# A hybrid attention trunk on one core: two groups of transposes move from TensorE to VectorE, two small matmul runs are merged, and one decay step is cut into even pieces

## The chip, the core and the metric

One core of a Trainium2 chip runs the whole kernel as one program. The metric is the device time of one execution in microseconds (us), median of several runs. TensorE is the matrix engine (PE in the rows, its weight loads PEld), VectorE is DVE, ScalarE is ACT, GpSimd is POOL, SyncE (SP) issues the weight DMAs. SBUF is the on-chip memory of 128 partitions, PSUM the accumulator memory that TensorE writes.

## What is computed

Batch 1, 256 tokens, width 2048, one layer, all in 32-bit floats. Cut to what matters:

```
h = rmsnorm(x);  z = h @ w_in         # q,k,v,gates of three branches, merge gates
a = gated linear attention (4 heads, key 128, value 256, chunked, key-wise decay)
a = rmsnorm(a) * silu(gate_a)          # 256 x 1024: "the gated attention's output"
b = forgetting attention (8 heads of 64, softmax with a forget bias) * silu(gate_b)
c = attention into 256 memory tokens (4 heads of 128) * silu(gate_c)
y = sum over the 3 branches of sigmoid(merge_i) * (branch_i @ w_branch_i)   # 256 x 2048
x = x + y @ w_out;  out = rmsnorm(x)
```

A matmul here takes its left operand with the contracted dimension on the partitions, so `a` and `y`, which come out with the tokens on the partitions, have to be transposed before they are multiplied by w_branch and w_out.

## The kernel before

**The stream.** Every large product is a stream of weight blocks of 2048 x 512 (`ORDER`). A block comes in 4 DMAs of 1 MB (`raw`), and is used in 8 pieces of 2 k-tiles. Each piece is split in two: ScalarE casts `hi` (line 173), VectorE subtracts to get `lo` (line 186), and TensorE forms hi*h1 + lo*h1 + hi*h2 in the format fp32r (lines 223 to 225 in `natural`, 253 and 258 in `transposed`, 1119 to 1121 for w_out). In `natural` a k-tile takes 6 matmuls of 512 columns, a piece 12. `w_kts` writes the cast of piece n+3 and the subtraction of piece n+2 into the program when TensorE's piece n comes; `hi` and `lo` have 4 buffers each.

**The lanes.** All other work is written as Python generators in three lists, `post`, `side` and `main`. After every k-tile `pull()` takes one step of the first generator in each list, so a step's instructions stand between two k-tiles in the order of every engine; `yield n` skips n-1 pulls, and `gap(n)` is a generator that only waits n pulls. Engines run their own instructions in this written order and wait for each other by semaphores.

**The places that the change touches.**
- `gla_scores` (from line 587): the key-wise decay is handled in three steps of block sizes 32, 8, 2. In the first one (`li == 0`) the scores of one 128-token block are three products with 32 rows each and 96, 64 and 32 columns (line 732), each in its own 32-column strip of the array; the later steps have four products of 48 columns. VectorE and ScalarE copy the results to `gA` (line 751).
- `fox` (from line 787): the forgetting attention goes over pairs of heads in a pipeline: `scores` (line 806, contraction 64, so half of the array's rows), softmax, `trans` (line 830, TensorE transposes), `moved` (line 834, VectorE copies to SBUF), `values` (line 842, 64 output rows, so half of the array's columns).
- `to_T` (line 921): for the two 512-wide halves of the gated attention's output `G["o"]`, eight times two TensorE transposes of 128 x 128 into PSUM (line 930), then ScalarE (933) and VectorE (934) make the two parts of `oT`. It runs in `post` right behind the gate of its half.
- `y_to_T` (line 1020): per 512-wide block n of y, two groups of four TensorE transposes (line 1030), then ScalarE (1032) and VectorE (1033) make the two parts of `yT`. It runs in `post` while the next block's first merge gate streams; the last one runs while w_out streams.
- `memory` (line 871), which is not changed, runs beside the first `to_T`: per head scores (904), maximum (906), exponential (910), norm (913, 915), transposes (895), copy (899), values (886).

Of the kernel before, what the change touches and what calls it, by code (L numbers as in the profile page):

```python
# [48 lines left out]
C_GAIN, C_MGAIN, C_BGK, C_GLAG, C_BF, C_N = 0, 16, 32, 36, 38, 39  # L49
# [10 lines left out]
def body(ctx, tc, xw, memT, xn, memn, wall, wsm, wup, cst, fgain, out):  # L60
    nc = tc.nc
    MM = nc.tensor.matmul
# [27 lines left out]
    def att():  # L90
        return ps_att.tile([P, NB], F32, tag="att", name=nm("att"))
# [27 lines left out]
    def gap(n):  # L119
        yield n  # L120
# [73 lines left out]
    def w_block():  # L194
        i = nblk[0]
        nblk[0] += 1
        return i

    def w_kts(i, group=1):

        for p in range(8):
            n = 8 * i + p
            if p % group == 0:
                w_cast(n + 3)
            if group == 1:
# [249 lines left out]
    G = {}  # L455
# [147 lines left out]
    def gla_scores():  # L603
# [79 lines left out]
        ps = att()  # L683
# [7 lines left out]
        for li in range(len(STEPS) + 1):  # L691
            s = STEPS[li] if li < len(STEPS) else None
            Qs = []
            if s:
                E = prep_keys(s)
                yield 2
                nc.scalar.activation(E, E, AF.Exp, scale=1.0 / 16)
                Qs.append(prep_queries(s, 0))
                yield 2
                nc.vector.tensor_tensor(out=E, in0=E, in1=gkf, op=ALU.mult)  # L700
                nc.scalar.activation(Qs[0], Qs[0], AF.Exp, scale=1.0 / 16)
                yield 2
                Qs.append(prep_queries(s, 1))
                yield 2
                nc.scalar.activation(Qs[1], Qs[1], AF.Exp, scale=1.0 / 16)
                times_q(Qs[0], s, 0)
                yield 2
                times_q(Qs[1], s, 1)
                yield 3
            else:  # L710
                E = gkf
                for half in range(2):
                    Qs.append(prep_pairs(half))
                yield 2
                for half in range(2):
                    nc.scalar.activation(odd(Qs[half]), odd(Qs[half]), AF.Exp, scale=1.0 / 16)
                yield 2
                for half in range(2):
                    times_odd(Qs[half], half)
                yield 2  # L720

            if li == 0:
                pss = [att().rearrange("p (e i) -> p e i", e=4) for _ in range(2)]
                off, n_q = (0, 96, 160), 3
            else:
                ps = att()[:, :8 * 48].rearrange("p (e i) -> p e i", e=8)
                off, n_q = (0, 48, 96, 144), 4
            for e in range(8):
                for j in range(n_q):
                    n = 96 - 32 * j if li == 0 else 48  # L730
                    dst = pss[e // 4][:, e % 4, P - n:] if li == 0 else ps[:, e, :]
                    MM(dst[32 * j:32 * j + 32], lhsT=E[:, e * P + 32 * j:e * P + 32 * j + 32],  # L732
                       rhs=Qs[e // 4][:, e % 4, off[j]:off[j] + n], start=True, stop=True,
                       skip_group_check=True)
            if li == 0:
                places = []
            elif s:
                m = gmask[li - 1][:, :, :8 // s or 1]
                places = [(gD.rearrange("p e (b s) -> p e b s", s=4 * s)[:, :, :, (b + 1) * s:],
                           m[:, b:b + 1, :].unsqueeze(3),  # L740
                           ps[:, :, (0, 24, 40)[b]:(24, 40, 48)[b]].rearrange("p e (b s) -> p e b s", s=(3 - b) * s))
                          for b in range(3)]
            else:
                places = [(gD.rearrange("p e (b s) -> p e b s", s=2)[:, :, :, 1], gpair[:, :, :16], ps[:, :, :16]),
                          (gD, gdiag[:, :, :32], ps[:, :, 16:])]
            yield 1
            if li == 0:
                for j in range(3):
                    q = slice(32 * j, 32 * j + 32)
                    for c in range(2):  # L750
                        (nc.scalar.copy if j == 1 else nc.vector.tensor_copy)(
                            gA[q, 4 * c:4 * c + 4, q.stop:], pss[c][q, :, q.stop:])
            for dst, mask, src in places:
                nc.vector.copy_predicated(dst, mask.bitcast(U32).to_broadcast(list(src.shape)), src)
            yield 2
# [34 lines left out]
    def fox():  # L790
# [45 lines left out]
        def values(p):  # L836

            po = att()
            for a, b, j, sl in ((0, S, 0, slice(0, S)), (P, S, 1, slice(S, 3 * P))):
                for e in range(2):  # L840
                    h = 2 * p + e
                    MM(po[64 * e:64 * e + 64, a:b], lhsT=fv[:, j, h * 64:(h + 1) * 64], rhs=pts[h][:, sl],
                       start=(j == 0), stop=(j == 1), skip_group_check=True)
            return po


        for k in range(6):
            this, last = (2 * k, 2 * k + 1), (2 * k - 2, 2 * k - 1)
            if k >= 2:
                po = values(k - 2)  # L850
                yield 1
                nc.scalar.copy(ob[:, k - 2, :], po[:, :S])
            if 1 <= k < 5:
                for h in last:
                    trans(h)
                yield 1
                for h in last:
                    moved(h)
                yield 1
            if k < 4:  # L860
                scores(k)
                yield 1
                for h in this:
                    masked(h)
                yield 1
                for h in this:
                    exps(h)
                yield 2
                for h in this:
                    normed(h)  # L870
                yield 2


    def memory():
# [43 lines left out]

    oT = [None] * 4

    def to_T(first, src, gain):

        for c in range(4):
            ct = first + c
            g, k = ct // 4, ct % 4
            if oT[g] is None:
                oT[g] = hpool.tile([P, 4, 2, S], F32R, tag=f"m12_{g}", name=nm("oT"))
            ps = att()
            for t in range(NT):
                nc.tensor.transpose(ps[:, t * P:(t + 1) * P], src(c, t), ident)  # L930
            yield 1
            sc = gain(c)
            nc.scalar.activation(oT[g][:, k, 0, :], ps[:, :S], AF.Copy, scale=sc)
            nc.vector.scalar_tensor_tensor(out=oT[g][:, k, 1, :], in0=ps[:, :S], scalar=sc,
                                           in1=oT[g][:, k, 0, :].bitcast(F32), op0=ALU.mult, op1=ALU.subtract)

    def silu_gate(dst, rstd):

# [69 lines left out]
    for cc in range(2):  # L1008
        gate = silu_gate(lambda t, cc=cc: G["o"][t][:, cc * NB:(cc + 1) * NB],
                         lambda cc=cc: G["rstd"][:, :, 2 * cc:2 * cc + 2])  # L1010
        post.append(gate)
        post.append(to_T(4 * cc, lambda c, t, cc=cc: G["o"][t][:, cc * NB + c * P:cc * NB + (c + 1) * P],
                         gain=lambda c: cs[:, C_GLAG + c % 2:C_GLAG + c % 2 + 1]))
    silu_gate_T("ob", 2)
    silu_gate_T("om", 3)
    main.drain()
# [4 lines left out]
    def y_to_T(n, y):  # L1021
        yield 2
        for c2 in range(2):
# [3 lines left out]
            for c in range(2):  # L1027
                for t in range(NT):
# [4 lines left out]
            nc.vector.tensor_tensor(out=yt[:, :, 1, :], in0=ps, in1=yt[:, :, 0, :].bitcast(F32),  # L1033
                                    op=ALU.subtract)

    def open_gate(ps, gt_):
        for t in range(NT):
            yield 1
            nc.scalar.activation(gt_[:, t, :], ps[t], AF.Sigmoid, scale=xcol[:, t:t + 1])
# [10 lines left out]
    for n in range(4):  # L1050
        gates = []
        for br in range(3):
            ps = natural(x12, range(KT), w_kts(w_block()))
            gates.append(a4([P, NT, NB]))
            post.append(open_gate(ps, gates[br]))
        src = w_kts(w_block())
        for br in range(3):
            kts = BR_KT[br]
            ps = natural(oT, kts, (next(src) for _ in kts))
            post.append(gated(br, ps, gates[br], gates[0]))  # L1060
        yT.append([])
        post.append(y_to_T(n, gates[0]))


    xr = []
# [189 lines left out]
```

## Time and profile before

| | |
|---|---|
| three runs | 803.58, 803.72, 804.22 us; median 803.72 |
| the profiled execution | 803.53 us |
| its span (first to last instruction) | 801.8 us, so 1.7 us lie around it |
| busy share of the span | TensorE 99%, weight loads 83%, VectorE 61%, ScalarE 51%, GpSimd 2% |
| TensorE's granted clock | 0.997 of full speed (2.4 GHz) over the span |
| chain that ended last | TensorE 95%, VectorE 2%, ScalarE 1% |
| DMA | 158.9 MB, mean 198 GB/s |

Busy time of TensorE is modelled as overlapping: a matmul of 512 columns is shown with 0.39 us, yet the next one starts 0.23 us later. So this document prices TensorE's work by distances between starts. Some matmuls stand twice in the trace: one of plain 32-bit operands is recorded as two.

### The profile page before, as it was taken

The page shows a single profiled execution, that of the slowest core. Times are in us where ns is not written, and L with a number is a line of the kernel's source. Part 1 is how long each engine was busy: PE and PEld are TensorE (multiplying, and loading weights), DVE is VectorE, ACT ScalarE, POOL GpSimd, SP SyncE. Part 2 cuts the span into 40 slices and gives each one's busy share as a digit, 9 for nine tenths or more (in the row PEclk, how much of TensorE's full clock was granted, in tenths as well). Part 3 has the DMA queues.
Part 4 walks back from the last instruction along what each step waited for, and adds up shares of the span by engine and source line. Part 5 has one row for each costly group of instructions (what it writes and reads, how often), then busy time and mean ns, then how long its engine had stood idle before and what let it go on. Part 6 is the DMA issues. An engine that isn't in the chain of part 4 may idle for free.

```text
span 801.8 us, 10259 instructions
## 1 busy us (share of the span) xinstructions
PE 792.7 (99%) x4064; PEld 663.5 (83%) x4064; DVE 486.7 (61%) x667; ACT 406.5 (51%) x562; POOL 15.3 (2%) x33
## 2 busy tenths in 40 slices
PE   9999999999999999999999999999999999999996
PEld 7888888888888788888888888888888888888886
DVE  6767978854757476676446644564447544575653
ACT  6768665654445475655444444444444444444632
POOL 5000000001000000000000000000000000000000
PEclk9999999999999999999999999999999999999998
DMA  9955747555544444455565565564555555548632
GB/s 325 387 200 184 251 163 296 168 205 185 204 158 158 158 158 158 158 203 185 190 209 182 186 202 176 200 208 165 204 198 177 204 182 188 207 164 296 248 132 106
DMA packets 27072, 158.90 MB, mean 198 GB/s; under 512 B 2984, under 2 KB 4528, under 8 KB 10128
## 3 DMA queue, kind: packets, MB, share of 16 engines
q1 hardware_dynamic: 26880, 158.22, 56.4%
q8 instruction: 32, 0.52, 0.3%
q14 instruction: 16, 0.13, 0.1%
q10 hardware_dynamic: 144, 0.02, 0.0%
HBM read 156.13 MB, written 2.11 MB: 197 GB/s over the span
## 4 chain that ended last, share of the span: by engine, by line
PE 95%; DVE 2%; ACT 1%; issue 1%; DMA 0%; SPq 0%; DVEq 0%
PE acc L223 19%; PE acc L225 19%; PE acc L224 19%; PE acc L253 13%; PE acc L258 7%; PE acc L1120 4%; PE acc L1119 4%; PE acc L1121 4%; PE att L253 2%; PE att L258 1%; DVE lo L186 1%; PE att L732 0%; PE att L442 0%; DMA xw<-xw 0%; PE att L1030 0%
## 5 line engine op out<-in xcount | busy, mean ns | idle before, releaser
L186 DVE TENSOR_TENSOR lo<-raw,hi 128x1024 fp32r<-128x1024 f32 x256 | 312.0, 1222 | 204.6 <-ACT hi L173 204.4
L173 ACT CAST hi<-raw 128x1024 fp32r<-128x1024 f32 x256 | 266.4, 1052 | 308.9 <-PE acc L225 239.9
L223 PE MATMUL acc<-hi,x 128*128 128x512 f32 x544 | 214.5, 394 | 0.0
L224 PE MATMUL acc<-lo,x 128*128 128x512 f32 x544 | 212.0, 390 | 0.0
L225 PE MATMUL acc<-hi,x 128*128 128x512 f32 x544 | 212.0, 390 | 0.0
L225 PEld LDWEIGHTS acc<-hi,x 128*128 128x128 f32 x544 | 102.1, 188 | 21.6
L223 PEld LDWEIGHTS acc<-hi,x 128*128 128x128 f32 x544 | 102.2, 188 | 21.1 <-issue 0.7
L224 PEld LDWEIGHTS acc<-lo,x 128*128 128x128 f32 x544 | 102.2, 188 | 20.8 <-DVE lo L186 0.4
L253 PE MATMUL acc<-x,hi 128*128 128x512 f32 x384 | 107.1, 400 | 0.0
L253 PEld LDWEIGHTS acc<-x,hi 128*128 128x128 f32 x384 | 66.3, 189 | 10.7 <-issue 1.0
L258 PEld LDWEIGHTS acc<-x,lo 128*128 128x128 f32 x384 | 58.8, 189 | 8.2
L258 PE MATMUL acc<-x,lo 128*128 128x256 f32 x384 | 61.0, 280 | 0.0
L225 PE MATMUL acc<-hi,oT 128*128 128x512 f32 x128 | 49.8, 389 | 0.0
L224 PE MATMUL acc<-lo,oT 128*128 128x512 f32 x128 | 49.8, 389 | 0.0
L223 PE MATMUL acc<-hi,oT 128*128 128x512 f32 x128 | 49.8, 389 | 0.0
L1119 PE MATMUL acc<-hi,a 128*128 128x512 f32 x96 | 37.5, 391 | 0.0
L1121 PE MATMUL acc<-hi,a 128*128 128x512 f32 x96 | 37.4, 389 | 0.0
L1120 PE MATMUL acc<-lo,a 128*128 128x512 f32 x96 | 37.4, 389 | 0.0
L223 PEld LDWEIGHTS acc<-hi,oT 128*128 128x128 f32 x128 | 24.0, 188 | 5.0
L224 PEld LDWEIGHTS acc<-lo,oT 128*128 128x128 f32 x128 | 24.0, 188 | 5.0
L225 PEld LDWEIGHTS acc<-hi,oT 128*128 128x128 f32 x128 | 24.0, 188 | 5.0
L1121 PEld LDWEIGHTS acc<-hi,a 128*128 128x128 f32 x96 | 18.0, 188 | 3.8
(222 smaller groups left out, 726.2 us busy)
## 6 DMA issues: line engine op xcount, KB each, us to landing
raw<-wall SPq DMA_DIRECT2D x130, 1024.0 KB, 4.8
a<-xn SPq DMA_DIRECT2D x8, 512.0 KB, 8.9
xw<-xw SPq DMA_DIRECT2D x4, 768.0 KB, 6.6
xw<-xw SPq DMA_DIRECT2D x7, 384.0 KB, 5.6
a<-memT SPq DMA_DIRECT2D x4, 512.0 KB, 5.8
a<-memn SPq DMA_DIRECT2D x4, 512.0 KB, 7.4
lraw<-wall SPq DMA_DIRECT2D x2, 1024.0 KB, 8.0
out<-a SPq DMA_DIRECT2D x8, 256.0 KB, 2.5
```

Of the source, the lines that this page charges most:

```text
L173: nc.scalar.copy(hi, raws[q][:, 2 * s:2 * s + 2, :])
L186: nc.vector.tensor_tensor(out=lo, in0=raws[q][:, 2 * s:2 * s + 2, :], in1=parts[n][0].bitcast(F32), op=ALU.subtract)
L223: MM(ps[t], lhsT=h1, rhs=hi, start=(kt == first), stop=False)
L224: MM(ps[t], lhsT=h1, rhs=lo, start=False, stop=False)
L225: MM(ps[t], lhsT=h2, rhs=hi, start=False, stop=(kt == last))
L253: MM(ps[c], lhsT=hi[:, c * P:(c + 1) * P], rhs=h_of(h, kt).rearrange("p a s -> p (a s)"), start=(kt == 0), stop=False, skip_group_check=True)
L258: MM(ps[c][:, :S], lhsT=lo[:, c * P:(c + 1) * P], rhs=h_of(h, kt)[:, 0, :], start=False, stop=(kt == KT - 1), skip_group_check=True)
L1119: MM(ps, lhsT=h1, rhs=hi, start=(kt == 0), stop=False)
L1120: MM(ps, lhsT=h1, rhs=lo, start=False, stop=False)
L1121: MM(ps, lhsT=h2, rhs=hi, start=False, stop=(kt == KT - 1))
```

## The change

Four edits. (1) `to_T` no longer uses TensorE: VectorE transposes 32 x 32 squares from SBUF to SBUF, 16 instructions per token tile of 128, so 32 per half and 64 in all (each 32 partitions x 4 squares, 128 elements per partition); the lines that make `oT` then read SBUF. It now runs in `side`, 10 pulls behind its gate, two squares per pull. (2) For y blocks 0 to 2 `y_squares` does the same with 16 instructions per block (32 partitions x 8 squares, 256 elements), one per pull, in `main`, 10 pulls after the block's end; block 3 keeps TensorE. (3) `fox`: `values` of pair k-2 now stands right in front of `scores` of pair k, behind `trans` and `moved`. (4) The first decay step's three products of 96, 64, 32 columns become four of 64, 64, 32, 32: the last 32 columns of the first go into the fourth strip.

```diff
             if li == 0:
                 pss = [att().rearrange("p (e i) -> p e i", e=4) for _ in range(2)]
-                off, n_q = (0, 96, 160), 3
+                todo = [(0, 0, 32, 96, 0), (1, 1, 64, P, 96), (2, 2, 96, P, 160), (3, 0, 96, P, 64)]
             else:
                 ps = att()[:, :8 * 48].rearrange("p (e i) -> p e i", e=8)
-                off, n_q = (0, 48, 96, 144), 4
+                todo = [(j, j, 0, 48, 48 * j) for j in range(4)]
             for e in range(8):
-                for j in range(n_q):
...
+                for j, k, a, b, off in todo:
+                    dst = pss[e // 4][:, e % 4, a:b] if li == 0 else ps[:, e, :]
+                    MM(dst[32 * j:32 * j + 32], lhsT=E[:, e * P + 32 * k:e * P + 32 * k + 32],
+                       rhs=Qs[e // 4][:, e % 4, off:off + b - a], start=True, stop=True,
                        skip_group_check=True)
...
         for k in range(6):
             this, last = (2 * k, 2 * k + 1), (2 * k - 2, 2 * k - 1)
-            if k >= 2:
-                po = values(k - 2)
-                yield 1
-                nc.scalar.copy(ob[:, k - 2, :], po[:, :S])
             if 1 <= k < 5:
                 for h in last:
                     trans(h)
@@
                 for h in last:
                     moved(h)
                 yield 1
+            if k >= 2:
+                po = values(k - 2)
             if k < 4:
                 scores(k)
-                yield 1
+            yield 1
+            if k >= 2:
+                nc.scalar.copy(ob[:, k - 2, :], po[:, :S])
+            if k < 4:
                 for h in this:
                     masked(h)
...
-                yield 2
+                yield 3 if k >= 2 else 2
...
+    def squares_T(dst, src, kts, ts):
+        v = src.rearrange("p t (k c i) -> p k t c i", c=4, i=32)
+        u = dst.rearrange("p k (t r j) -> p k t r j", r=4, j=32)
+        for r in range(4):
+            for c in range(4):
+                nc.vector.transpose(u[32 * c:32 * c + 32, kts, ts, r, :], v[32 * r:32 * r + 32, kts, :, c, :])
+                yield 1
+
+    def to_T(g, gain):
+        z = a4([P, 4, S])
+        for t in range(NT):
+            for i, _ in enumerate(squares_T(z, G["o"][t][:, g * NB:(g + 1) * NB].unsqueeze(1), slice(0, 4),
+                                            slice(t, t + 1))):
+                if i % 2:
+                    yield 1
...
-        post.append(to_T(4 * cc, lambda c, t, cc=cc: ...
+        side.append(gap(10))
+        side.append(to_T(cc, lambda c: cs[:, C_GLAG + c % 2:C_GLAG + c % 2 + 1]))
...
+    def y_squares(n, y):
+        z = a4([P, 4, S])
+        yield from squares_T(z, y, slice(0, 4), slice(0, NT))
+        for c2 in range(2):
...
+        if n == 0:
+            side.drain()
...
-        post.append(y_to_T(n, gates[0]))
+        if n < 3:
+            main.append(gap(10))
+            main.append(y_squares(n, gates[0]))
+        else:
+            post.append(y_to_T(n, gates[0]))
```

**TensorE's order in `fox`, pair k = 3.** Before, `values` of pair 1 (L842) stands eight stream matmuls ahead of `trans` of pair 2 (L830), and `scores` of pair 3 (L806) comes twelve stream matmuls behind that:

```order
L842 MATMUL att_2429<-b_2326,a_1767 64x256
L842 MATMUL att_2429<-b_2328,a_1767 64x256
L842 MATMUL att_2429<-b_2326,a_1767 64x128
L842 MATMUL att_2429<-b_2328,a_1767 64x128
L253 MATMUL acc_2255<-x_35_261,hi_2330 128x512 x2
L253 MATMUL acc_2255<-x_35_261,hi_2332 128x512 x2
L258 MATMUL acc_2255<-x_35_261,lo_2348 128x256 x2
L258 MATMUL acc_2255<-x_35_261,lo_2378 128x256 x2
L830 MATMUL att_2449<-ident,b_2358 128x128 x3
L830 MATMUL att_2453<-ident,b_2362 128x128 x3
```

Now the two stand together, behind `trans`:

```order
L225 MATMUL acc_2466<-hi_2406,x_6_116 128x512
L842 MATMUL att_2479<-b_2318,a_1777 64x256
L842 MATMUL att_2479<-b_2320,a_1777 64x256
L842 MATMUL att_2479<-b_2318,a_1777 64x128
L842 MATMUL att_2479<-b_2320,a_1777 64x128
L806 MATMUL att_2484<-a_1280,a_1029 128x128
L806 MATMUL att_2485<-a_1280,a_1029 128x128
L806 MATMUL att_2484<-a_1280,a_1029 128x256
L806 MATMUL att_2485<-a_1280,a_1029 128x256
L223 MATMUL acc_2465<-hi_2406,x_6_116 128x512
```

Nothing of the stream stands between `values` and `scores` any more. The number of matmuls is the same, and it is so for two pairs, k = 2 and k = 3. The second `scores` matmul takes a PSUM buffer that the first of the two `moved` copies (VectorE) frees.

**VectorE's order beside the memory attention**, from the middle of the fourth gate block (`lo` is the stream's subtraction L186, `a_1878`/`a_1888` and `a_1879`/`a_1889` the two halves of the attention's output, `msum` and `mmx` the memory attention's sums and maxima). Before:

```order
L186 TENSOR_TENSOR lo_2944<-raw_2793,hi_2930 128x1024
L957 TENSOR_TENSOR a_1878<-a_1878,b_2882 128x512
L186 TENSOR_TENSOR lo_2971<-raw_2793,hi_2932 128x1024
L957 TENSOR_TENSOR a_1879<-a_1879,b_2883 128x512
L899 COPY b_2984<-att_2966 128x512
L906 TENSOR_REDUCE mmx<-att_2986 128x2
L907 TENSOR_SCALAR mmx<-mmx 128x2
L186 TENSOR_TENSOR lo_3008<-raw_2845,hi_2990 128x1024
L934 SCALAR_TENSOR_TENSOR oT_3002<-att_3003,cs,oT_3002 128x256
L934 SCALAR_TENSOR_TENSOR oT_3002<-att_3020,cs,oT_3002 128x256
L186 TENSOR_TENSOR lo_3038<-raw_2845,hi_2992 128x1024
```

Now, the same stretch:

```order
L186 TENSOR_TENSOR lo_2956<-raw_2794,hi_2940 128x1024
L930 STREAM_TRANSPOSE a_2802<-a_1889 32x4x32 x2
L970 TENSOR_TENSOR a_1888<-a_1888,b_2884 128x512
L930 STREAM_TRANSPOSE a_2802<-a_1889 32x4x32 x2
L186 TENSOR_TENSOR lo_2987<-raw_2794,hi_2942 128x1024
L970 TENSOR_TENSOR a_1889<-a_1889,b_2885 128x512
L930 STREAM_TRANSPOSE a_2802<-a_1889 32x4x32 x2
L901 COPY b_3002<-att_2982 128x512
L930 STREAM_TRANSPOSE a_2802<-a_1889 32x4x32 x2
L908 TENSOR_REDUCE mmx<-att_3004 128x2
L909 TENSOR_SCALAR mmx<-mmx 128x2
L186 TENSOR_TENSOR lo_3024<-raw_2843,hi_3008 128x1024
```

Two squares stand between nearly every two of the old instructions. From the copy of the second head's transposes to the last subtraction of this weight block there are 20 of them, and 28 in the second half's stretch, from the first to the last subtraction of the first merge block.

## Rows read from the trace of the kernel before

**Rows 1.** The page: busy time, share of the span and instructions of each engine; and the chain of work that ended last, shares of the span by engine.

```profile
PE 792.7 (99%) x4064; PEld 663.5 (83%) x4064; DVE 486.7 (61%) x667; ACT 406.5 (51%) x562; POOL 15.3 (2%) x33
...
PE 95%; DVE 2%; ACT 1%; issue 1%; DMA 0%; SPq 0%; DVEq 0%
```

**Rows 2.** All waits of TensorE in the span: who was waited for, us in total, times, longest.

```profile
PE att L354 <- DVE ones L346: 1.1, 1, 1.1
PE att L253 <- DVE x L360: 0.5, 1, 0.5
```

**Rows 3.** The page's groups of the stream's two preparing instructions: out<-in, sizes, count | busy us, mean ns of one | idle time of the engine just before them, and what ended most of it.

```profile
L186 DVE TENSOR_TENSOR lo<-raw,hi 128x1024 fp32r<-128x1024 f32 x256 | 312.0, 1222 | 204.6 <-ACT hi L173 204.4
L173 ACT CAST hi<-raw 128x1024 fp32r<-128x1024 f32 x256 | 266.4, 1052 | 308.9 <-PE acc L225 239.9
```

**Rows 4.** Timeline of TensorE around the first four transposes of y block 0: start us, duration us, instruction, count.

```profile
448.62 0.39 PE L223 MATMUL acc<-hi,x 128*128 128x512 f32 x1
...
450.43 0.39 PE L225 MATMUL acc<-hi,x 128*128 128x512 f32 x1
450.66 0.60 PE L1030 MATMUL att<-ident,a 128*128 128x128 f32 x4
...
451.33 0.40 PE L224 MATMUL acc<-lo,x 128*128 128x512 f32 x1
```

**Rows 5.** The same around the first two transposes of the gated attention's output.

```profile
291.06 0.39 PE L225 MATMUL acc<-hi,x 128*128 128x512 f32 x1
291.29 0.38 PE L930 MATMUL att<-ident,a 128*128 128x128 f32 x2
...
291.74 0.40 PE L224 MATMUL acc<-lo,x 128*128 128x512 f32 x1
```

**Rows 6.** Timeline of TensorE at the first decay step (columns 96, 64, 32; the row names the first form) and at the second (columns 48), each with the stream's next matmuls.

```profile
110.17 1.51 PE L732 MATMUL att<-a,a 128*32 128x96 f32 x48
111.60 1.21 PE L253 MATMUL acc<-x,hi 128*128 128x512 f32 x4
...
134.25 0.89 PE L732 MATMUL att<-a,a 128*32 128x48 f32 x64
135.07 0.98 PE L253 MATMUL acc<-x,hi 128*128 128x512 f32 x3
```

**Rows 7.** Timeline of TensorE around one run of `scores` (L806) and one of `values` (L842) in the forgetting attention.

```profile
236.67 0.64 PE L258 MATMUL acc<-x,lo 128*128 128x256 f32 x4
237.14 1.09 PE L253 MATMUL acc<-x,hi 128*128 128x512 f32 x4
238.07 0.63 PE L258 MATMUL acc<-x,lo 128*128 128x256 f32 x4
238.63 0.93 PE L806 MATMUL att<-a,a 64*128 64x128 f32 x8
...
247.54 0.64 PE L258 MATMUL acc<-x,lo 128*128 128x256 f32 x4
248.10 0.87 PE L842 MATMUL att<-b,a 128*64 128x256 f32 x8
248.91 1.20 PE L253 MATMUL acc<-x,hi 128*128 128x512 f32 x4
```

**Rows 8.** Timeline at pair k = 3: VectorE's two copies of the transposes (L834), and TensorE's next `scores`.

```profile
251.95 1.01 DVE L834 COPY b<-att 128x384 f32<-128x384 f32 x2
...
253.91 0.93 PE L806 MATMUL att<-a,a 64*128 64x128 f32 x8
```

**Rows 9.** VectorE's groups by shape, for prices: 128, 256, 512 and 1024 elements per partition with two tensors read, then a copy of 32 partitions and a scaling by a column, both of 256 elements.

```profile
L639 DVE TENSOR_TENSOR a<-a 128x128 f32<-128x128 f32 x6 | 1.7, 286 | 0.0
L639 DVE TENSOR_TENSOR a<-a 128x256 f32<-128x256 f32 x6 | 2.5, 418 | 0.0
L1044 DVE TENSOR_TENSOR a<-acc,a 128x512 f32<-128x512 f32 x24 | 16.4, 683 | 0.0
L628 DVE TENSOR_TENSOR a<-a 128x1024 f32<-128x1024 f32 x3 | 3.7, 1219 | 0.0
L758 DVE COPY a<-b 32x256 f32<-32x256 f32 x2 | 0.6, 279 | 0.0
L915 DVE TENSOR_SCALAR b<-b,msum 128x256 f32<-128x256 f32 x8 | 2.5, 351 | 0.1
```

**Rows 10.** Timeline of VectorE: two such copies in a row, which write different groups of 32 partitions, and two such scalings in a row, which write all 128.

```profile
174.12 0.57 DVE L758 COPY a<-b 32x256 f32<-32x256 f32 x2
...
296.84 0.62 DVE L915 TENSOR_SCALAR b<-b,msum 128x256 f32<-128x256 f32 x2
```

**Rows 11.** VectorE's busy time in two stretches: from, to; length, busy us, instructions; then granted clock, DMA share, GB/s.

```profile
302.00:324.00 22.00, 14.46 (x24) 1.00 0.37 137
348.00:369.50 21.50, 15.37 (x16) 1.00 0.58 196
```

**Rows 12.** Timeline: the last subtraction of the fourth gate block (VectorE) and its first use (TensorE, L258); the last subtraction of the first merge block (the first of two in its row) and its first use (TensorE, L224).

```profile
322.81 1.22 DVE L186 TENSOR_TENSOR lo<-raw,hi 128x1024 fp32r<-128x1024 f32 x1
324.78 0.40 PE L258 MATMUL acc<-x,lo 128*128 128x256 f32 x2
...
368.41 2.35 DVE L186 TENSOR_TENSOR lo<-raw,hi 128x1024 fp32r<-128x1024 f32 x2
373.36 0.39 PE L224 MATMUL acc<-lo,x 128*128 128x512 f32 x1
```

More of the change, by code (lines that the diff above doesn't have):

```diff
@@ L723, in gla_scores @@
                 pss = [att().rearrange("p (e i) -> p e i", e=4) for _ in range(2)]
-                off, n_q = (0, 96, 160), 3
+                todo = [(0, 0, 32, 96, 0), (1, 1, 64, P, 96), (2, 2, 96, P, 160), (3, 0, 96, P, 64)]
             else:
                 ps = att()[:, :8 * 48].rearrange("p (e i) -> p e i", e=8)
-                off, n_q = (0, 48, 96, 144), 4
+                todo = [(j, j, 0, 48, 48 * j) for j in range(4)]
             for e in range(8):
-                for j in range(n_q):
[L730 to L733, printed above, removed]
+                for j, k, a, b, off in todo:
+                    dst = pss[e // 4][:, e % 4, a:b] if li == 0 else ps[:, e, :]
+                    MM(dst[32 * j:32 * j + 32], lhsT=E[:, e * P + 32 * k:e * P + 32 * k + 32],
+                       rhs=Qs[e // 4][:, e % 4, off:off + b - a], start=True, stop=True,
                        skip_group_check=True)
@@ L747, in gla_scores @@
             if li == 0:
-                for j in range(3):
-                    q = slice(32 * j, 32 * j + 32)
+                for j, k, a, b, _ in todo:
                     for c in range(2):
-                        (nc.scalar.copy if j == 1 else nc.vector.tensor_copy)(
-                            gA[q, 4 * c:4 * c + 4, q.stop:], pss[c][q, :, q.stop:])
+                        (nc.scalar.copy if j % 2 else nc.vector.tensor_copy)(
+                            gA[32 * k:32 * k + 32, 4 * c:4 * c + 4, a:b], pss[c][32 * j:32 * j + 32, :, a:b])
             for dst, mask, src in places:
@@ L919, in body @@
     oT = [None] * 4
-    def to_T(first, src, gain):
-        for c in range(4):
[L924 to L930, printed above, removed]
+    def squares_T(dst, src, kts, ts):
[12 more added lines that the diff above has]
+                    yield 1
+        oT[g] = hpool.tile([P, 4, 2, S], F32R, tag=f"m12_{g}", name=nm("oT"))
+        for c in range(4):
+            sc = gain(c)
+            nc.scalar.activation(oT[g][:, c, 0, :], z[:, c, :], AF.Copy, scale=sc)
             yield 1
[L932 to L935, printed above, removed]
+            nc.vector.scalar_tensor_tensor(out=oT[g][:, c, 1, :], in0=z[:, c, :], scalar=sc,
+                                           in1=oT[g][:, c, 0, :].bitcast(F32), op0=ALU.mult, op1=ALU.subtract)
+            yield 1
     def silu_gate(dst, rstd):
@@ L1011, in body @@
         post.append(gate)
-        post.append(to_T(4 * cc, lambda c, t, cc=cc: G["o"][t][:, cc * NB + c * P:cc * NB + (c + 1) * P],
-                         gain=lambda c: cs[:, C_GLAG + c % 2:C_GLAG + c % 2 + 1]))
+        side.append(gap(10))
+        side.append(to_T(cc, lambda c: cs[:, C_GLAG + c % 2:C_GLAG + c % 2 + 1]))
     silu_gate_T("ob", 2)
@@ L1034, in y_to_T @@
                                     op=ALU.subtract)
+    def y_squares(n, y):
+        z = a4([P, 4, S])
+        yield from squares_T(z, y, slice(0, 4), slice(0, NT))
+        for c2 in range(2):
+            yt = a4([P, 2, 2, S], F32R)
+            yT[n].append(yt)
+            nc.scalar.copy(yt[:, :, 0, :], z[:, 2 * c2:2 * c2 + 2, :])
+            yield 1
+            nc.vector.tensor_tensor(out=yt[:, :, 1, :], in0=z[:, 2 * c2:2 * c2 + 2, :],
+                                    in1=yt[:, :, 0, :].bitcast(F32), op=ALU.subtract)
+            yield 1
     def open_gate(ps, gt_):
```

## The prediction

> **What bounds the kernel now.** I read the busy shares and the chain first. TensorE is busy for 792.7 of 801.8 us and makes up 95% of the chain that ended last [rows 1]. The view of waits is next: in the whole span TensorE waits twice, 1.1 and 0.5 us, both in the first microseconds [rows 2]. So nobody makes TensorE wait, and every instruction taken out of its queue shortens the run by its distance to the next start, as long as the others still keep up. Do they have room? The stream's cast on ScalarE has 308.9 us of idle time before it, most of it until TensorE frees a buffer, and the subtraction on VectorE 204.6 us, until that cast is done [rows 3]. Both follow TensorE and do not lead it. VectorE, which gets the new work, is busy 61% of the span [rows 1], but that is a mean; what counts are the two stretches in which `to_T` now runs beside the memory attention and beside the last gates.
>
> The time sum below is made against the profiled execution, 803.53 us; the median of the three runs shown is 0.19 us above it, and the forecast is given for the median. About 0.2%, or 1.6 us, is what a measurement of this kernel can tell from no change.
>
> **What leaves TensorE.** Busy times overlap, so I price by starts. From the start at 448.62 to that at 450.66 there are nine steps of the stream [rows 4], so an ordinary one takes 0.227 us.
> - *y, blocks 0 to 2.* From the L225 before four transposes to the second matmul behind them it is 451.33 - 450.43 = 0.90 us [rows 4]; two ordinary steps are 0.453, so the four cost 0.447, which contains a late start of the matmul behind them. Six such groups go: **2.68 us**.
> - *The gated attention's output.* The same with two transposes: 291.74 - 291.06 - 0.453 = 0.227 us [rows 5], eight groups: **1.81 us**.
> - *First decay step.* Its run takes 111.60 - 110.17 = 1.43 us for 8 blocks of 96, 64 and 32 columns, 0.179 each; the next step takes 135.07 - 134.25 = 0.82 us for 8 blocks of four times 48, 0.1025 each [rows 6]. Both have 192 columns per block, so the sum of columns does not set the time, the widest strip does: 0.0016 us per column. A widest strip of 64 gives 0.128 us, 8 blocks 1.02: **0.41 us** saved. Bounds: 0, if the width does not matter between the two, and 0.61, if 64, 64, 32, 32 runs like four times 48. A loss by the higher count (32 matmuls for 24) is excluded by the second run, which has 32 and is shorter. One evacuation more per half falls to ScalarE, which is 51% busy.
> - *`values` and `scores` together, twice.* A run of half-array matmuls starts late and lets the stream start late. `scores` comes at 238.63; the four L258 ahead of it, from 238.07, would let the next matmul start after 0.47 us, as in the group before, so 0.09 us are lost. Behind `values` four L253 last 1.20 us in place of 1.09, 0.11 lost [rows 7]. Two runs lose 0.40 us, four such switches. Together, two of them become one, between half the columns and half the rows, which no row shows. If it is free, 0.20 us a pair; if it costs as much as leaving and coming back, 0. I take the nearest row, the 0.09 of one entry, so 0.1 a pair: **0.21 us** with both (0.0 to 0.40; a loss of another 0.2 if that switch costs two more entries).
>
> The Trainium skill (TensorEngine Tiling (Array Packing), Key Properties) says that a change of tiling mode, not of the tile, drains TensorE. By that rule the merged run still drains once in the middle and the pair saves one drain of three or four, the 0.1 taken above; a reader who expects both to vanish would put 0.40 into the sum. The 0.09 and 0.11 us of the rows agree with a drain at every change.
>
> The new wait in this edit: the second `scores` matmul waits for the first `moved` copy. At k = 3 both copies are over at 252.96 and `scores` comes at 253.91 [rows 8]; the copies stand as far ahead of it as before, so nothing. Behind it the whole stream would wait.
>
> Sum: 2.68 + 1.81 + 0.41 + 0.21 = **5.1 us**.
>
> **What VectorE gets, and what covers it.** No row shows a transpose on VectorE. Its 64 squares of 128 elements and 48 of 256 are bounded below by the copy of 32 partitions, 0.28 us for 256, and above by a row of twice the elements, 0.42 and 0.68 us; I take the rows of the same size that read at one element a cycle, 0.29 and 0.42 us [rows 9], nearer since nothing is computed. Two scalings of 0.351 take 0.62 us together, 0.08 less than their sum, but two copies that write different 32 partitions take 0.57, just twice 0.279 [rows 10]: squares change the written partitions each time, so I count them in full. That is 64 x 0.29 + 48 x 0.42 = 38.7 us, on an engine with 315 us to spare. It costs nothing where the subtraction of a piece still ends before TensorE uses it. Three places:
> - *y.* One square per pull, two per piece. A piece takes TensorE 12 x 0.227 = 2.72 us, VectorE 1.22 + 0.84 = 2.06. Covered, also at 0.68 (2.58).
> - *First half*, beside the memory attention. From 302 to 324.0, where the gate block's last subtraction ends, VectorE is busy 14.46 of 22.0 us, 7.5 idle [rows 11]; it gets 20 squares, 5.8 us, and two old scalings (1.0) move out. Adding up the new order from the copy at 302 on, with the old waits for TensorE kept and 0.08 us overlap between other instructions, I get the last subtraction ready some 2 us before TensorE asks. Before, that was 324.78 - 324.03 = 0.75 [rows 12], held up by scalings that waited for ScalarE. The cover lasts to 0.29 + 2/20 = 0.39 us a square.
> - *Second half*, beside the first merge gate. From 348 to 369.5 it is busy 15.37, 6.1 idle [rows 11]. The old subtraction ends at 369.6 and is used at 373.36 [rows 12], 3.8 to spare. 28 squares at 0.29 are 8.1 us, 2.0 more than the idle time: 1.8 remain. The cover lasts to 0.35.
>
> Behind these squares ScalarE's first `oT` instruction waits for the last square, with the casts of the next pieces behind it; those casts are written three pieces ahead, 8.2 us, and the squares end about when the old `oT` work did. `oT` and `yT` are needed blocks later. SP's and GpSimd's instructions keep their order. So the second term is 0, **803.72 - 5.1 = 798.6 us**.
>
> **The rivals.**
> - *B: squares at half the rate*, 0.42 and 0.68 us. For: nothing measured here excludes it. Against: a row of equal size exists for every other operation. Then the first half overruns by 20 x 0.13 - 2 = 0.6 and the second by 28 x 0.13 - 1.8 = 1.8, TensorE waits 2.4 us for `lo` there, and the time is 801.0.
> - *C, the slow side: VectorE becomes the bound at the squares.* TensorE loses 48(p - 0.29) - 3.8 us in the two stretches, with p the price of the small square. It decides from p = 0.48 on, where that eats 5.1. At a quarter of the rate, with the rows of four times the elements, 0.68 and 1.22 [rows 9], the stretches lose 14.9, and each y block 16 x 1.22 less the 8 x 1.50 us that VectorE has free beside the pieces, less 3.8 of lead: 3.7, three times 11. The time is 803.7 - 5.1 + 26 = 825. Against: twice to four times the price of anything of this size in the rows. The Trainium skill (VectorE: DVE Perf Modes, Rules for kernel authors) would have a 128 x 128 transpose on TensorE when a PSUM destination will do, and so speaks against the whole change; in this trace TensorE is the engine without free time [rows 1], which speaks for it. Its section on the three transpose paths gives 0.311 us for 128 x 128 of bf16 on VectorE; by that estimate the small square stays under both limits above.
> - *D: nothing is won.* The time taken out of TensorE comes back as waits for casts or weights, since a producer was just as close. Time 803.7. For: the share of DMA and the 83% of weight loads. Against: two waits in 800 us [rows 2] and ScalarE idle until TensorE frees buffers [rows 3]. That the squares replace nothing is excluded by the program's order.
>
> **How the numbers follow.** Forecast 80%: 798.6, with its own range 797.7 (0.9 more, from the two merged terms at their upper bounds and the groups a little dearer than shown) to 799.6 (decay and merge at 0, and a few tenths of waits). B 9%, at 801.0. C 5%. D 6%. The range of 8 in 10 takes in the forecast and B: 797.6 to 801.2, leaving out C, D and some of the edges. Faster by over 0.2% (below 802.1) is the forecast and most of B, 0.88; within it D and the rest of B, 0.07; slower C, 0.05.
>
> **What would show it.** In the profile after: TensorE's records fall from 4064 to 4040 (40 transposes less, 16 records more in the decay step); its waits stay at the two of now; the first decay run takes about 1.0 us; `values` and `scores` have one gap of about 0.1 between them; squares have means near 0.29 and 0.42. The prediction is wrong if TensorE shows waits for `lo` (L186) near 320 or 370, or if the squares are over 0.36. Squares at 0.3 with a time over 800 would mean that TensorE's instructions did not give back their starts.

## The result, and the profile after

| | before | after |
|---|---|---|
| median of the runs taken side by side | 803.97 us (803.58 to 804.22, 4 runs) | **799.49 us** (799.18 to 799.82, 4 runs) |
| ratio | | 0.9945, 95% interval 0.9928 to 0.9962 |
| profiled execution, its span | 803.53, 801.8 us | 799.18, 797.5 us |

The forecast was 798.6 us, with a range of 797.6 to 801.2. The time fell by 4.5 us where 5.1 were expected; the granted clock is 0.997 as before. Two views of the page after, which answer to [rows 1] and [rows 3]: busy time by engine with the chain, and the groups of the stream's two preparing instructions.

```profile
PE 787.8 (99%) x4040; PEld 659.0 (83%) x4040; DVE 527.5 (66%) x779; ACT 406.1 (51%) x564; POOL 15.2 (2%) x33
...
PE 92%; DVE 4%; ACT 2%; issue 1%; DMA 0%; SPq 0%; DVEq 0%; ACTq 0%
...
L186 DVE TENSOR_TENSOR lo<-raw,hi 128x1024 fp32r<-128x1024 f32 x256 | 312.3, 1223 | 171.2 <-ACT hi L173 169.8
L173 ACT CAST hi<-raw 128x1024 fp32r<-128x1024 f32 x256 | 266.3, 1052 | 302.8 <-PE acc L225 221.1
```

TensorE's records fell to the 4040 forecast. VectorE took on 41 us and still has 171 us of idle time before its subtractions. By these rows nothing is short. But VectorE's part of the chain doubled, and TensorE's waits, which answer to [rows 2], have a new line:

```profile
PE att L354 <- DVE ones L346: 1.1, 1, 1.1
PE acc L224 <- DVE lo L186: 0.7, 1, 0.7
PE att L253 <- DVE x L360: 0.4, 1, 0.4
```

TensorE waits once for `lo`: the sign that the prediction named as its failure. The timeline of TensorE at that place, the first merge block:

```profile
367.78 0.39 PE L223 MATMUL acc<-hi,x 128*128 128x512 f32 x1
368.19 0.50 PE L224 MATMUL acc<-lo,x 128*128 128x512 f32 x1
...
370.83 0.39 PE L223 MATMUL acc<-hi,x 128*128 128x512 f32 x1
371.97 0.50 PE L224 MATMUL acc<-lo,x 128*128 128x512 f32 x1 [0.74 <-DVE lo L186]
372.30 0.39 PE L225 MATMUL acc<-hi,x 128*128 128x512 f32 x1
```

Starts 0.41 and 1.14 us apart stand where 0.227 is usual, and the next step is each time 0.11 late as well: 0.29 and 1.02 us, **1.3 us** lost. Only the larger of the two got into the view of waits, with less than its length. VectorE in the same stretch (start us, duration us, instruction, count):

```profile
365.00 1.23 DVE L985 TENSOR_TENSOR a<-a,a 128x1024 f32<-128x1024 f32 x1
366.26 0.62 DVE L930 STREAM_TRANSPOSE a<-a 32x128 f32<-32x128 f32 x2
366.91 1.23 DVE L186 TENSOR_TENSOR lo<-raw,hi 128x1024 fp32r<-128x1024 f32 x1
368.17 0.61 DVE L930 STREAM_TRANSPOSE a<-a 32x128 f32<-32x128 f32 x2
368.80 1.23 DVE L990 TENSOR_TENSOR oT<-a,oT 128x1024 fp32r<-128x1024 f32 x1
370.04 0.62 DVE L930 STREAM_TRANSPOSE a<-a 32x128 f32<-32x128 f32 x2
370.69 1.23 DVE L186 TENSOR_TENSOR lo<-raw,hi 128x1024 fp32r<-128x1024 f32 x1
371.94 1.26 DVE L930 STREAM_TRANSPOSE a<-a 32x128 f32<-32x128 f32 x4
```

No row has an idle note: VectorE is the bound here. The subtractions end at 368.14 and 371.92, TensorE starts 0.05 us behind each. Over the two stretches that [rows 11] showed, moved to their new places, VectorE's busy time is:

```profile
299.50:322.00 22.50, 20.23 (x42) 1.00 0.35 130
345.10:371.95 26.85, 24.57 (x46) 1.00 0.46 157
```

A view of groups by shape gives the new prices (busy us, mean ns | idle before):

```profile
L930 DVE STREAM_TRANSPOSE a<-a 32x256 f32<-32x256 f32 x48 | 20.9, 436 | 1.0
L930 DVE STREAM_TRANSPOSE a<-a 32x128 f32<-32x128 f32 x64 | 19.3, 302 | 1.1
```

### The profile page after: what moved, and what is told of

Read it like the earlier page. It is cut to its first block, busy times and chain, and to the rows that moved or that the text cites. A ratio compares the mean times of both kernels' runs of the same rounds, so it can differ in the third digit from the quotient of the medians.

```text
span 797.5 us, 10329 instructions
## 1 busy us (share of the span) xinstructions
PE 787.8 (99%) x4040; PEld 659.0 (83%) x4040; DVE 527.5 (66%) x779; ACT 406.1 (51%) x564; POOL 15.2 (2%) x33
## 4 chain that ended last, share of the span: by engine, by line
PE 92%; DVE 4%; ACT 2%; issue 1%; DMA 0%; SPq 0%; DVEq 0%; ACTq 0%
PE acc L223 18%; PE acc L224 18%; PE acc L225 18%; PE acc L253 13%; PE acc L258 7%; PE acc L1152 4%; PE acc L1151 4%; PE acc L1150 4%; PE att L253 2%; DVE lo L186 1%; PE att L258 1%; DVE a L930 1%; PE att L442 0%; DMA xw<-xw 0%; PE att L733 0%
## 5 line engine op out<-in xcount | busy, mean ns | idle before, releaser
L186 DVE TENSOR_TENSOR lo<-raw,hi 128x1024 fp32r<-128x1024 f32 x256 | 312.3, 1223 | 171.2 <-ACT hi L173 169.8
L224 PE MATMUL acc<-lo,x 128*128 128x512 f32 x544 | 212.1, 390 | 0.8 <-DVE lo L186 0.7
L224 PEld LDWEIGHTS acc<-lo,x 128*128 128x128 f32 x544 | 102.2, 188 | 22.6 <-DVE lo L186 2.0
L258 PEld LDWEIGHTS acc<-x,lo 128*128 128x128 f32 x384 | 58.8, 189 | 8.2
L258 PE MATMUL acc<-x,lo 128*128 128x256 f32 x384 | 61.0, 281 | 0.0
L224 PE MATMUL acc<-lo,oT 128*128 128x512 f32 x128 | 49.8, 389 | 0.0
L930 DVE STREAM_TRANSPOSE a<-a 32x128 f32<-32x128 f32 (+1 forms) x112 | 40.2, 359 | 2.1
L224 PEld LDWEIGHTS acc<-lo,oT 128*128 128x128 f32 x128 | 24.0, 188 | 5.0
```

What stands on the lines that cost most here:

```text
L186: nc.vector.tensor_tensor(out=lo, in0=raws[q][:, 2 * s:2 * s + 2, :], in1=parts[n][0].bitcast(F32), op=ALU.subtract)
L224: MM(ps[t], lhsT=h1, rhs=lo, start=False, stop=False)
L258: MM(ps[c][:, :S], lhsT=lo[:, c * P:(c + 1) * P], rhs=h_of(h, kt)[:, 0, :], start=False, stop=(kt == KT - 1), skip_group_check=True)
L930: nc.vector.transpose(u[32 * c:32 * c + 32, kts, ts, r, :], v[32 * r:32 * r + 32, kts, :, c, :])
```

## The experiments

**Theory A**: TensorE gets back what left its queue, and the 1.3 us are VectorE's second half, too full since a square takes more of VectorE than its own duration: the instruction in front of it loses its overlap. **Rivals**: the waits come of something else (the y squares, weights), the taken-out instructions are worth less than their starts, or the busy share of VectorE sets a limit.

**The second half's squares later.**

```diff
-        side.append(gap(10))
+        side.append(gap((10, 26)[cc]))
```

> The changed kernel with the second half's squares put 16 pulls later (a gap of 26 in place of 10), so that they run beside the first and second merge gates, where VectorE has little but the subtractions. Theory A (the 1.3 us that TensorE waits for lo near 368 and 372 us are an overrun of VectorE beside the last gate's own work): both waits vanish, the median is 1.3 us below the changed kernel's, about 798.2, and the span about 796.2. Theory B (the squares cost TensorE time wherever they stand, because VectorE falls behind the stream by their sum): the waits move along with them and the time stays at 799.5. Theory C (the wait comes from ScalarE's casts, which stand behind an instruction that waits for the squares): the same move helps only if no cast stands behind the later squares; the casts stand behind them there too, so the waits stay at about 1 us.

798.10 us (797.70 to 799.43, 5 runs), ratio to before 0.9933 (0.9919 to 0.9946). TensorE's waits:

```profile
PE att L354 <- DVE ones L346: 1.1, 1, 1.1
PE att L253 <- ACT hi L129: 0.8, 1, 0.8
PE att L253 <- DVE x L360: 0.5, 1, 0.5
```

Only first-microsecond waits are left. The same squares, put where the stretch has room, cost nothing: theory A.

**Groups of four squares, every second pull**, so the same squares with half as many neighbours.

```diff
-                if i % 2:
-                    yield 1
+                if i % 4 == 3:
+                    yield 2
```

> The changed kernel with the squares of the gated attention's output in groups of four every second pull, in place of two every pull: the same squares in the same stretch, but half as many places where a square stands beside another instruction. Theory A1 (a pair of squares takes about 0.65 us from start to start, and the instruction ahead of it loses its 0.08 to 0.12 us of overlap, so a junction costs more than a square's own 0.30): with 14 pairs made into 7 groups in the second half's stretch, VectorE needs about 7 x 0.12 = 0.8 us less, and TensorE's waits fall from 1.3 to about 0.4 us: 798.6. Theory A2 (only the squares' own durations count, 28 x 0.30 against the free time): the waits stay within 0.2 us of 1.3, and the time at 799.5.

798.58 us (798.49 to 799.01, 5 runs), ratio 0.9936 (0.9924 to 0.9949), no wait for `lo` in the view; by starts, 0.2 of the 1.3 us remain. VectorE at the place:

```profile
368.94 1.23 DVE L990 TENSOR_TENSOR oT<-a,oT 128x1024 fp32r<-128x1024 f32 x1
370.08 1.22 DVE L186 TENSOR_TENSOR lo<-raw,hi 128x1024 fp32r<-128x1024 f32 x1
371.33 1.26 DVE L930 STREAM_TRANSPOSE a<-a 32x128 f32<-32x128 f32 x4
372.62 1.23 DVE L186 TENSOR_TENSOR lo<-raw,hi 128x1024 fp32r<-128x1024 f32 x1
```

`oT` to `lo` is 1.14 us, they overlap; `lo` to a square is 1.25. Neither the number of squares nor their durations changed, and 1.1 of the 1.3 us went, somewhat more than the 0.8 that seven junctions were to give: the price is at the junctions.

**The two together.**

```diff
-                if i % 2:
-                    yield 1
+                if i % 4 == 3:
+                    yield 2
...
-        side.append(gap(10))
+        side.append(gap((10, 26)[cc]))
```

> The second half's squares 16 pulls later and the squares in groups of four at every second step, together. Theory A: each alone already takes the waits for lo away (798.1 and 798.6 us), so both together give nothing more: 798.1 (797.7 to 798.5), ratio 0.993, no wait for lo. If the waits were not all that VectorE costs TensorE here, the fewer junctions would give more on top of the later start, below 797.6.

798.12 us (797.81 to 799.79, 5 runs), ratio 0.9934 (0.9921 to 0.9948). Nothing on top: once `lo` is in time, VectorE costs TensorE nothing.

**The parts.** y alone (parts 1, 3 and 4 undone):

```diff
-        side.append(gap(10))
-        side.append(to_T(cc, ...
+        post.append(to_T(4 * cc, ...
```

> The kernel before with the squares for y blocks 0 to 2 alone; the gated attention's output, the decay step and the forgetting attention are as before. If the gain of this part is the distance between TensorE's starts, with VectorE covering the 48 squares, the time is 2.7 us below before, 801.2, and TensorE waits nowhere for lo. If the squares of 0.44 us put VectorE behind in the merge gates, it is less than 2 us below.

801.07 us (800.70 to 801.78, 5 runs), ratio 0.9967 (0.9955 to 0.9980); no wait for `lo`. The attention's output alone (parts 2, 3 and 4 undone):

```diff
-        if n < 3:
-            main.append(gap(10))
-            main.append(y_squares(n, gates[0]))
-        else:
-            post.append(y_to_T(n, gates[0]))
+        post.append(y_to_T(n, gates[0]))
```

> The kernel before with the squares for the gated attention's output alone. TensorE loses 16 transposes, 1.8 us. Theory A: the waits of 1.3 us near 370 us come with it and with nothing else, so the time is only 0.5 us below before, 803.4. If the waits need the other edits too (a schedule shifted by the merged runs), it is 1.8 us below, 802.1.

803.50 us (803.12 to 804.91, 11 runs), ratio 1.0001 (0.9993 to 1.0010): no difference. In its profiled execution, TensorE gets 1.8 us back and gives 1.4 away at 370.5 and 374.3, so the waits belong to this part. The half microsecond that should remain is less than the medians can tell, and that execution lost 1.5 us in its first microseconds. The decay step and the merged runs alone (parts 1 and 2 undone):

```diff
-        side.append(gap(10))
-        side.append(to_T(cc, ...
+        post.append(to_T(4 * cc, ...
...
-            main.append(y_squares(n, gates[0]))
...
+        post.append(y_to_T(n, gates[0]))
```

> The kernel before with the two small edits alone: the first decay step in four even strips, and values and scores together for two pairs of heads. Theory A (each run's saving is a distance between TensorE's starts and comes back in full): the decay step gives 0.42 us, and the two merged runs give 0.39 us if the change from half the columns to half the rows is free in the middle of a run; 0.8 us below before, 802.9. If only one entry is saved per pair, 0.6 us below. Theory B (small runs are hidden by something else): no change.

802.95 us (802.65 to 803.33, 11 runs), ratio 0.9987 (0.9978 to 0.9996). Differences to each one's own before: 2.65, 0.22 and 1.06 us, sum 3.9, against 4.5 for the whole; the intervals allow that. The traces settle it, from a mark behind the first microseconds, in which the profiled executions differ by up to 1.5 us: from the last weight matmuls ahead of the first decay step to TensorE's last start. Before, then after:

```profile
109.60 0.64 PE L258 MATMUL acc<-x,lo 128*128 128x256 f32 x4
794.05 0.28 PE L1121 MATMUL acc<-last,a 128*128 128x256 f32 x1
...
109.70 0.64 PE L258 MATMUL acc<-x,lo 128*128 128x256 f32 x4
789.91 0.28 PE L1152 MATMUL acc<-last,a 128*128 128x256 f32 x1
```

That is 684.45 us before and 680.21 after, 4.24 less. Between the same two matmuls y alone takes 2.88 us less than before, the attention's output alone 0.44, the two small edits 0.92: together 4.24, so the parts add up and neither help nor hinder each other.

**The loops of the squares exchanged**, to see whether the change of the read or of the written partitions makes the junction.

```diff
-        for r in range(4):
-            for c in range(4):
+        for c in range(4):
+            for r in range(4):
```

> The changed kernel with the two loops over squares exchanged: four squares in a row now write the same 32 partitions and read four different groups, in place of the reverse. Theory A (two squares do not overlap because any change of the partition group, read or written, makes the next one wait): starts stay 0.325 us apart for the small squares. Theory B (only a change of the written group does that): three of four squares start about 0.08 us earlier, 0.24 us apart, and TensorE's waits near 370 us shrink from 1.3 us to nothing.

One run, 799.44 us; means 302 and 436 ns, pairs 0.65 us from start to start, the wait for `lo` 0.8. Either change has the same price.

**The y squares three times** (each square is written three times in a row, to the same place with the same values).

```diff
-        yield from squares_T(z, y, slice(0, 4), slice(0, NT))
+        for _ in zip(*[squares_T(z, y, slice(0, 4), slice(0, NT)) for _ in range(3)]):
+            yield 1
```

> The changed kernel with each square of y blocks 0 to 2 written three times in a row (the same values each time), so VectorE gets six squares per piece in place of two. Theory A (cover is free time plus lead: a square costs 0.46 us from start to start, a subtraction 1.26; a piece takes TensorE 2.72 us, VectorE now 4.0, so 1.3 us are missing in each of 8 pieces, 10.3 per block, less a lead of about 4 us): TensorE waits some 6 us for lo in each of three blocks, and the time is about 818. Theory B (VectorE can be overrun only by what its whole-kernel busy share says, which would be 71%): 799.5.

One run, 813.81 us. The view of waits, then VectorE in block 0:

```profile
PE acc L224 <- DVE lo L186: 11.8, 13, 1.1
```

```profile
463.99 1.22 DVE L186 TENSOR_TENSOR lo<-raw,hi 128x1024 fp32r<-128x1024 f32 x1
465.24 2.77 DVE L930 STREAM_TRANSPOSE a<-a 32x256 f32<-32x256 f32 x6
468.05 1.23 DVE L186 TENSOR_TENSOR lo<-raw,hi 128x1024 fp32r<-128x1024 f32 x1
```

A piece takes VectorE 4.06 us, TensorE 2.72: over 8 pieces 10.7 us are missing. By TensorE's starts a block loses 4.9 us, so some 5.8 us are lead, more than the 4 that I had assumed. Cover is idle time plus lead: the mean busy share, 70% here, tells nothing of it.

**What merging costs: the two heads' matmuls of `values` and `scores` alternated.** In each merged run, seven changes between half the columns and half the rows instead of one.

```diff
-            if k >= 2:
-                po = values(k - 2)
-            if k < 4:
-                scores(k)
+            both = []
+            if k >= 2:
+                po = att()
+                both.append(values(k - 2, po))
+            if k < 4:
+                both.append(scores(k))
+            for _ in range(5):
+                for run in both:
+                    next(run, None)
```

where `scores` and `values` have become generators that yield after each matmul.

> The changed kernel with the four matmuls of values and the four of scores of a pair written alternately, one of each in turn, in the two merged runs. The rows of the changed kernel's merged run show no gap at its one change from half the columns to half the rows. Theory A (a change between these two shapes costs nothing, only the change from or to whole-array matmuls does): each run still takes 1.66 us, the time stays at 799.5. Theory B (each change of the array's tiling drains it, 0.09 us or more, and the one change was hidden by chance): six more changes in each of two runs, so a run takes 2.2 us or more, the time 800.6 or more. A gain would mean that the two shapes partly run beside each other.

804.09 us (803.85 to 805.12, 10 runs), ratio 1.0002 (0.9993 to 1.0011): 4.6 us more than the whole change, and neither number. The first merged run in the changed kernel:

```profile
235.93 0.87 PE L842 MATMUL att<-b,a 128*64 128x256 f32 x8
236.74 0.93 PE L806 MATMUL att<-a,a 64*128 64x128 f32 x8
237.59 1.20 PE L253 MATMUL acc<-x,hi 128*128 128x512 f32 x4
```

and alternated (each matmul of plain 32-bit operands is two records):

```profile
235.95 0.65 PE L842 MATMUL att<-b,a 128*64 128x256 f32 x2
236.53 0.48 PE L806 MATMUL att<-a,a 64*128 64x128 f32 x2
236.94 0.65 PE L842 MATMUL att<-b,a 128*64 128x256 f32 x2
...
239.91 0.96 PE L253 MATMUL acc<-x,hi 128*128 128x512 f32 x3
```

1.66 us against 3.96. Alternating also parts the two heads of a pair, which take different halves of the array. So the next kernel keeps the heads next to each other.

**Pairs**: two of `values`, two of `scores`, and again; three changes. Against the alternating kernel:

```diff
                 for e in range(2):
...
-                    yield
+                yield
...
-            for _ in range(5):
+            for _ in range(3):
```

> In the two merged runs the matmuls stand as two of values, two of scores, two of values, two of scores: three changes of half instead of one, and the two heads of a pair stay next to each other. In the alternating order the run took 3.96 us in place of 1.66 with seven changes. Theory M, each change of half has a price: 2.30 us / 6 further changes = 0.38 each, so two further changes make the run 2.42 us, twice 0.77 more, 800.7 us, ratio to before 0.996. Theory L, what the alternating order lost is the overlap of the two heads' matmuls, which take different halves of the array: they stay neighbours here, the run takes 1.66 to 1.85 us (at most the 0.09 of an entry for each further change) and the time is 799.2 to 799.6, ratio 0.9945.

800.64 us (799.96 to 801.17, 5 runs), ratio 0.9958 (0.9945 to 0.9970). TensorE at the first merged run:

```profile
236.82 0.65 PE L842 MATMUL att<-b,a 128*64 128x256 f32 x4
237.40 0.49 PE L806 MATMUL att<-a,a 64*128 64x128 f32 x4
237.82 0.44 PE L842 MATMUL att<-b,a 128*64 128x128 f32 x4
238.19 0.70 PE L806 MATMUL att<-a,a 64*128 64x256 f32 x4
238.82 1.20 PE L253 MATMUL acc<-x,hi 128*128 128x512 f32 x4
```

The run takes 2.00 us, between the two theories, and the pieces decide. Two further changes cost 0.34 us, **0.17 us each**, which is theory M at half its price. Two heads together need 0.58 us for 256 columns of `values` up to the next start, one head alone needs 0.58 as well (rows above): side by side the second is free, which is theory L. Both had a part in the 2.3 us that alternating lost: its six further changes make 1.0 of them at 0.17 each, and the other 1.3 are then the second heads that no longer run beside the first. (The median says 1.15 us more than the whole change where two runs account for 0.7; in its profiled execution TensorE was 0.9 us later than in the changed kernel's within the first 12 us already, which is not of this edit.)

## Why the prediction was right, and the step that failed

- **y: right, a little small.** 2.68 forecast; the same distances at all six places give 2.71, and y alone measured 2.65 (the interval of the ratio is 1.6 to 3.6 us). In the traces it is worth 2.88: the next few steps of the stream behind each group were late as well, by a hundredth or less each ([rows 4] show only the first late start). The cover held: after each pair VectorE waits for the cast again, as the notes in its timeline show.

```profile
462.92 1.23 DVE L186 TENSOR_TENSOR lo<-raw,hi 128x1024 fp32r<-128x1024 f32 x1 [0.58 <-ACT hi L173]
464.18 0.88 DVE L930 STREAM_TRANSPOSE a<-a 32x256 f32<-32x256 f32 x2
465.64 1.23 DVE L186 TENSOR_TENSOR lo<-raw,hi 128x1024 fp32r<-128x1024 f32 x1 [0.58 <-ACT hi L173]
```

- **The attention's output: right on TensorE.** 1.81 forecast, 1.81 by starts.
- **Decay: right.** 64 columns in the widest strip take what the line between 48 and 96 gave, 1.02 us for the run ([rows 6] show the two others); 0.42 saved, 0.41 forecast:

```profile
110.26 1.09 PE L733 MATMUL att<-a,a 128*32 128x64 f32 x64
111.28 1.21 PE L253 MATMUL acc<-x,hi 128*128 128x512 f32 x4
```

- **The merge: mechanism right, size too small.** 0.39 us saved, its upper bound; I took 0.21. Before, the run of `values` took 0.81 us from its start to the stream's [rows 7], and that contains the change back to the whole array. In the merged run it is 0.81 again from `values` to `scores`: the change in the middle takes the place of that one. So a whole entry and the stream's late second step are saved, and I had charged one of them again. By the Trainium skill (TensorEngine Tiling (Array Packing), Key Properties) every change of mode drains; the 0.17 us per further change in the order by pairs agrees, so "no gap" in the merged run doesn't mean that the change is free.
- **VectorE's cover: the failed step.** "The cover lasts to 0.35" was sound; the price put against it was not. I had the durations almost right (0.302 and 0.436 against 0.29 and 0.42), but a pair of squares takes 0.65 from start to start, and costs the instruction ahead 0.12 of overlap: 0.77, or 0.385 a square, over that limit. 28 squares are 10.8 us, not 8.1: 2.7 more against 1.8 of margin. That gives 0.9 of overrun, measured 1.3. The other 0.4 is not accounted for by an experiment; but the margin took all 6.1 us of idle time as free, and in the stretch VectorE still waits 0.44, 0.37 and 0.66 us for ScalarE. The same price left the first half a margin of 0.4 us (the last `lo` ends at 321.77, TensorE uses it at 322.14), not 2.
- **The sum.** By the starts of the same matmuls in both traces TensorE got back 2.88 us from y, 1.81 from the attention's output, 0.42 from the decay step and 0.50 from the forgetting attention (0.1 of it from its last pairs, where nothing was forecast): 5.6 in place of 5.1. The waits for `lo` and small delays beside them took 1.4 away: 4.24. The profiled executions differ by 4.35: the first microseconds took 0.1 more than before, and 0.2 were won behind TensorE's last start, for a reason that no view here shows. So the time came close to the forecast in part by luck: the half microsecond that the forecast missed on TensorE's side hid part of what the second half lost. Rivals: D did not happen. B had the place of the second half right, but the first half did not overrun and the cause (half the rate) was another. C's cause, VectorE as the bound, is what happened in the second half, at an effective 0.385 us, well below the 0.48 from which C was to decide.

## What to carry to other kernels

An instruction put between others costs its distance from start to start and what its neighbours lose in overlap; price it by that, above all where 20 or 30 small ones fill a stretch, and compare with the idle time and lead of that stretch. A low mean busy share said nothing of the one stretch that was full, and moving the second half's squares by 16 steps was worth 1.4 us. Small parts add up in the traces when they are read from a mark behind the first microseconds, where medians can't separate them. When two runs that use part of the array meet, keep the matmuls that take different halves next to each other.

## What the runs showed of the hardware

**Which instructions overlap on VectorE.** The squares do it themselves, in the changed kernel's timeline of VectorE:

```profile
344.02 1.22 DVE L186 TENSOR_TENSOR lo<-raw,hi 128x1024 fp32r<-128x1024 f32 x1
345.16 0.61 DVE L930 STREAM_TRANSPOSE a<-a 32x128 f32<-32x128 f32 x2
346.21 1.23 DVE L186 TENSOR_TENSOR lo<-raw,hi 128x1024 fp32r<-128x1024 f32 x1 [0.44 <-ACT hi L173]
347.47 0.62 DVE L930 STREAM_TRANSPOSE a<-a 32x128 f32<-32x128 f32 x2
```

From `lo` to the first pair it is 1.14 us, to the second 1.26. The first pair begins with the square that reads and writes partitions 0 to 31, where `lo` begins too; the second begins with one that writes partitions 64 to 95. Over all 112 squares, the 7 which both read and write partitions 0 to 31 start 0.08 to 0.09 us before the instruction ahead ends; each of the other 105 starts 0.01 us or more after its end. The Trainium skill (VectorE: DVE Perf Modes, Two Vector instructions with no wait between them) has it so: an instruction is held until all earlier ones have finished when its output begins in another group of 32 partitions than the last output into the same memory, or an input in another group than the first input of the last instruction that read that memory. The trace agrees, by these two groups and by the exchanged loops. It is shown by comparison within a run, not by an edit of its own: the y squares written three times do keep both groups, but each repeat waits by a semaphore for the one before, which writes the same place, and starts 0.03 us after its end.

**Half-array matmuls.** Two heads in different halves cost the time of one, 0.58 us for 256 columns of `values` up to the next start; a change between half the columns and half the rows costs 0.17 us.
